# One split instruction a weight slab on ScalarE and one on VectorE, in place of two halves on each

## The chip, the cores and the metric

The kernel runs on one core of a Trainium2 chip. The metric is the device time of one launch in microseconds (us). Three launches of the kernel before were timed, and one execution was profiled.

## The reference

Two blocks of a network over 256 tokens with 1024 features each, in float32. What matters here is that nearly everything is a product of activations with a weight matrix that is used once, from an "even" mixer (attention and gated linear attention), a feed-forward unit (width 2816), an S5 mixer, eight experts of width 2816 (two for each token), and then the second block with another feed-forward unit, an SSD mixer, neighbourhood attention and per-layer embeddings:

```python
def adaln(c, w, b):
    m = jax.nn.silu(c.astype(jnp.float32)) @ w + b
    shift, scale, gate = jnp.split(m, 3, axis=-1)
    return shift[:, None, :], scale[:, None, :], gate[:, None, :]
...
def swiglu(h, w_gate, w_up, w_down):
    return (jax.nn.silu(h @ w_gate) * (h @ w_up)) @ w_down

def moe_swiglu(h, w_router, w_gate, w_up, w_down):
    logits = (h @ w_router).astype(jnp.float32)
    top_val, top_idx = lax.top_k(logits, TOP_K)
    weights = jax.nn.softmax(top_val, axis=-1)
    gates = jnp.sum(jax.nn.one_hot(top_idx, N_EXPERTS, dtype=jnp.float32) * weights[..., None], axis=-2)
    out = jnp.zeros_like(h)
    for e in range(N_EXPERTS):
        out = out + gates[..., e:e + 1] * swiglu(h, w_gate[e], w_up[e], w_down[e])
    return out
```

The products have to be as exact as float32 products.

## The kernel before

Activations lie with features on the 128 partitions and 256 tokens along the free axis. TensorE (PE) multiplies in the float32r type, so a float32 operand is cut into two parts, hi and lo (12 bits each, by the class's docstring), and each product is three matmuls (`mm3`: w hi by act hi, w hi by act lo, w lo by act hi).

The weights come through the class `Stream` as about 525 slabs of 128 x 2048 float32 (1 MB each), in the order of their use. A slab goes through three steps:

- `_load`: the SyncE queue (SP) issues a DMA into a raw buffer `wraw` (3 of them; during the experts 2 more, `wraw2`). A buffer is free for the next load when the split of the slab in it has read it for the last time.
- `_prep`: ScalarE (ACT) writes hi with an `activation` Copy, which rounds into the float32r tile `whi` (line 211), and VectorE (DVE) writes lo = raw - hi into `wlo` (line 212). Both are done in two halves of 1024 columns. There are 3 pairs of whi and wlo.
- the products (lines 269 and 271), in `proj`, `proj_tok`, `ffn`, `Down` and `moe_block`. Nearly all read a slab k by k, so that the first products need the first half of a slab alone.

The same engines do the rest of the work. In a feed-forward unit, each of 11 segments takes three slabs (gate g, up u and down d), and ACT and DVE make `gu` and its split `mh`, `ml` between the products. In the experts, each of 8 times 11 = 88 segments takes three slabs too. For segment s, PE makes the gate and up products, ACT the Silu `mt` (line 1655), DVE its product with up (line 1656), PE transposes it into `ms`, ACT and DVE split that into `mmh` and `mml` (lines 283 and 284), and PE makes the down products of the segment before. POOL has work in the mixers and at the ends of units.

The kernel is written in a framework that orders the instructions of each engine when the program is built: a planner with a clock of its own gives each engine's next place to the instruction of the highest priority among those that are ready by that clock. Priority is program order, moved by `high_priority(offset=...)`; `SPLIT_ORDER` moves the splits of some units by a few places. On the chip each engine then runs its list in that fixed order and waits, at each instruction, for what it depends on. An edit in `_prep` so changes what the planner sees for every slab. A name of a tile in the rows is that of the code; `hgx` is the activations that an expert works on.

Of the kernel before, what the change touches and what calls it, by code (L numbers as in the profile page):

```python
# [28 lines left out]
# How much earlier (or later) than in program order the parts of a weight slab are made, by the unit that takes it.  # L29
SPLIT_ORDER = {"s": -30, "f1_0": -100, "e": -200, "f2_0": 50}  # L30

# Vectors over features, one column of 128 partitions for each 128 features: name, input, columns.
# [10 lines left out]
def lay_out(inp):  # L43
    """The inputs as the kernel reads them: features on partitions, weights in the pieces that are loaded."""
    inp = {k: np.asarray(v) for k, v in inp.items()}

    def part(w, k=None):
        """[k * 128, n] -> [128, k, n]"""
        return w.reshape(-1, 128, w.shape[-1]).transpose(1, 0, 2)

    def cut(w, ranges):
        """columns of a matrix, 256 to a piece: [piece, 128, k, 256]"""
        return np.stack([part(np.concatenate([w[:, a:b] for a, b in r], 1)) for r in ranges])
# [4 lines left out]
    def tok(w, c0):  # L58
        """512 columns, in two pieces of 512 rows: [piece, 128, 4, 512]"""
        return np.stack([part(w[s * 512:(s + 1) * 512, c0:c0 + 512]) for s in range(2)])  # L60

    f = np.float32
# [26 lines left out]
    # columns on partitions: [piece, 128, 2, rows]  # L89
# [19 lines left out]
    # rpb[h, row distance, column distance] for each query column (twice, for two rows) and key column  # L109
# [7 lines left out]
def rows(w, k0, k1):  # L117
    """Rows of a matrix on partitions: [128, k1 - k0, columns]."""
    return w[k0 * 128:k1 * 128, :].rearrange("(k p) c -> p k c", p=128)
# [7 lines left out]
class Stream:  # L127
    """Weights in the order of their use. Loads run NR slabs ahead of the split into two
    float32r parts (exact: 12 + 12 bits), and the split runs NH slabs ahead of the products."""
# [19 lines left out]
    def grow(self, pool, n, until, limit=None):  # L149
        """n more loads at a time, into another pool, for what comes before slab (or key) `until`"""  # L150
        self.pool2, self.more, self.turn = pool, n, self.turn % self.NR
        self.until = until if isinstance(until, int) else self.key.get(until, len(self.plan))
        self.advance(limit)

    def once(self, pool, *names):
        """room for one more load each"""
# [37 lines left out]
    def _prep(self, i):  # L194
# [10 lines left out]
        m = n // 2  # L205
        k0 = self.plan[i][0]
        k0 = k0[0][0] if isinstance(k0[0], tuple) else k0[0]
        for c in range(0, n, m):
            cs = slice(c, c + m)
            with self.K.tc.high_priority(offset=SPLIT_ORDER[k0]) if k0 in SPLIT_ORDER else nullcontext():  # L210
                nc.scalar.activation(hi[:, cs], t[:, cs], AF.Copy)  # L211
                nc.vector.tensor_sub(lo[:, cs], t[:, cs], f32(hi[:, cs]))  # L212
# [34 lines left out]
class Kernel:  # L247
# [12 lines left out]
    # ------------------------------------------------------------ small helpers  # L260
# [3 lines left out]
    def first(self):  # L264
        """what comes within goes before other work that is ready at the same time"""
        return self.tc.high_priority(offset=200)
# [4 lines left out]
    def mm3(self, out, w, act, start, stop):  # L271
        """out += w.T @ act for float32 operands given as (high, low) float32r parts."""
# [4 lines left out]
    def tr(self, out, in_, o=0):  # L277
        """transpose of in_, whose first partition is o"""
# [10 lines left out]
    # ------------------------------------------------------------ constants  # L289
# [23 lines left out]
    # ------------------------------------------------------------ modulation  # L313
    def silu_row(self):
        """silu(c) as a row, on every partition"""
# [5 lines left out]
    def silu_c(self, pool):  # L321
        """silu(c) on partitions, each on its own with 31 columns of zeros, and room for partial sums"""
# [7 lines left out]
    def mod_plan(self, name, norm, part, pe):  # L330
        """shift | scale | gate of one sublayer: the matrix times silu(c), on PE with its rows on partitions (partial
        sums are then added over partitions on PE as well), or on DVE with its columns on partitions. part: which third."""
# [43 lines left out]
    def mod_flush(self, keep, norm=None):  # L376
        """what the last slabs of modulation matrices have left to do, but for the last few (and for what does not
        belong to that norm's first two thirds)"""
# [3 lines left out]
    def mod_next(self, n=None):  # L382
        """the next loads of modulation matrices go into the stream here"""
# [4 lines left out]
    # ------------------------------------------------------------ norms over features  # L388
# [5 lines left out]
    def norm_begin(self, pool=None):  # L394
        """pool: where a folded norm's h goes"""
# [4 lines left out]
    def sums(self, tag="ss"):  # L400
        """sums of squares of feature tiles: a tile, and those of the last pair, which are not added to it"""
        return [self.act.tile([128, T], F32, name=tag, tag=tag, bufs=1)]

    def sq_add(self, p, src, ss, gain=None, last=3):
        """adds the squares of two feature tiles (times a gain)"""
# [15 lines left out]
    def norm_part(self, p, g):  # L421
        """x[2p], x[2p+1] are final: their squares, and x * g in two parts"""
# [10 lines left out]
    def rstd_from(self, v, r):  # L433
        """r = 1 / sqrt(v), with one Newton step"""
# [14 lines left out]
    def col_sums(self, out, ss):  # L449
        """per token, tokens on partitions"""  # L450
# [5 lines left out]
    def rstd_cols(self, ss, n, b):  # L456
        """1 / rms of each token, tokens on partitions: [128, 2]"""
# [8 lines left out]
    def to_rows(self, r, b):  # L466
        """[128, 2] over tokens -> the same row of 256 tokens on every partition, in PSUM"""
# [18 lines left out]
    def mod_norm(self, norm, row=None, pre=None):  # L486
        """h = x * rstd * (gain * (1 + scale)) + shift, in two parts; squares were added up before. pre: products
        x * gain * (1 + scale) that were taken before"""
# [27 lines left out]
    # ------------------------------------------------------------ products  # L516
    def proj(self, keys, evac, k_outer=False, K=KD, act=None):
        """Columns of h @ w on partitions; evac(tile, out) per 128 columns, two tiles to a bank."""
# [26 lines left out]
    def proj_tok(self, keys, evac, act=None, per=4, mid=None):  # L545
        """h @ w with tokens on partitions, 512 columns: keys are slabs of `per` row tiles each; mid is called after the first."""
# [21 lines left out]
    class Down:  # L568
        """out.T over 8 feature tiles, accumulated over row tiles of w that come in pairs"""
# [22 lines left out]
    # ------------------------------------------------------------ residuals  # L592
# [13 lines left out]
    # ------------------------------------------------------------ feed forward  # L606
    def ffn_plan(self, key, gate, up, down, between=0, mid=None):
        """between: how many loads of modulation matrices go with each segment; mid: plans other work in the midst"""
# [14 lines left out]
    def ffn(self, key, tail, fold, end=None, mid=None):  # L623
        """fold: h is x * gain and 1/rms (from end) goes onto the products; else h is normalised"""
# [59 lines left out]
    # ------------------------------------------------------------ first block, layer 0: FoX + GLA  # L684
# [21 lines left out]
    def even_consts(self, pool, tmp):  # L706
        """Loads and masks of the mixer that wait for nothing"""
# [6 lines left out]
        # which head a row of the small product stands for  # L714
# [12 lines left out]
        # causal mask, to be added: 0 where s <= t, else very low  # L727
# [4 lines left out]
        # 1 where the running sum goes on, 0 where a chunk of 64 begins  # L732
# [4 lines left out]
        # level masks [s, t]: t in the second half of a block of 2m, s in the first half of the same one  # L737
# [8 lines left out]
        for i, sh in enumerate((6, 5, 4, 3, 2, 1, 0)):  # L746
            # t >> sh == (s >> sh) + 1 and (s >> sh) even  <=>  (t >> sh) ^ (s >> sh) == 1 and t > s
# [9 lines left out]
    def log_sigmoid(self, out, x, t, scale):  # L757
        """out = scale * log_sigmoid(x); t: a spare tile"""
# [7 lines left out]
    def even_mixer(self, pool, tail):  # L766
        nc, tc, E = self.nc, self.tc, self.E
        # the gates' small products first: their chain is the longest
# [26 lines left out]
        # log decays of GLA, summed within chunks of 64  # L795
# [11 lines left out]
        # FoX forget gates, summed over time  # L807
# [5 lines left out]
        # FoX queries and keys  # L813
# [10 lines left out]
        # GLA: decays between halves of blocks of 128, 64, ..., 2 steps, each from a point between the two,  # L824
        # so that no exponent is above 0
# [5 lines left out]
        def decay(m):  # L831
            """exp(-|b - b at the last step of the first half|)"""
# [42 lines left out]
        def lv_chunk():  # L875
            # over chunk boundaries: from the start of a later chunk, to the end of an earlier one
# [11 lines left out]
            # chunks 0, 1 -> 2, 3: also over the whole of chunk 1, of chunk 2  # L888
# [22 lines left out]
        # ---- FoX  # L911
# [3 lines left out]
        def fox_scores(hd):  # L915
# [12 lines left out]
            # minus the masked logits, and minus their maximum  # L928
# [56 lines left out]
        # ---- GLA out, normalised over its 128 features; the products of FoX's half with w_o come between  # L985
# [33 lines left out]
    # ------------------------------------------------------------ first block, layer 1: S5  # L1019
# [12 lines left out]
    def poly_exp(self, pool, x, out, m1=None):  # L1032
        """out = exp(x), m1 = exp(x) - 1, to float32's accuracy, for [128, 32] tiles"""
# [24 lines left out]
    def poly_trig(self, pool, th, sn, vs):  # L1058
        """sn = sin(th), vs = 1 - cos(th), for [128, 32] tiles"""
# [22 lines left out]
        for _ in range(2):  # L1082
            # sin 2y = 2 sin y (1 - v), 1 - cos 2y = 2 sin(y)^2
# [5 lines left out]
    def s5_tables(self, pool, rot, tmp):  # L1089
        """What depends on the parameters alone. State (g % 2, p) on partitions, pair g // 2 on columns."""  # L1090
# [15 lines left out]
        # a - 1 = (mag - 1) - mag (1 - cos)  # L1106
# [17 lines left out]
        # decay and turn of two steps  # L1124
# [16 lines left out]
        def cmul(pr_, pi_, xr, xi, cr, ci, neg=False):  # L1141
            """(pr, pi) = (xr, xi) * (cr, ci), the second over columns; neg: of conjugates"""
# [9 lines left out]
        # input weights f * b, and times a: [state, feature tile, re or im, pair, (a b, b), k]  # L1152
# [6 lines left out]
        # output weights re, -im, and those times a  # L1159
# [1349 lines left out]
```

## Time and profile before

| | |
|---|---|
| three launches | 2844.84, 2849.65 and 2849.4 us; median 2849.4 us |
| the profiled execution | span 2843.7 us; no device time of its own is listed, so what lies around its span is bounded by the launches: 1.1 to 6.0 us |
| PE, DVE, ACT, POOL busy | 2671.7, 2181.9, 1579.6 and 560.9 us |
| weight splits | 1046 instructions on ACT (1044.7 us) and 1046 on DVE (1282.3 us) |
| DMA | 623 MB, a mean of 219 GB/s |

Engines work side by side, so busy times don't add up to the span. A matmul's record and the next one's overlap, so PE's time is read from starts, not from durations. An engine that is idle costs nothing unless the work that ends last waits for it.

### The profile page before, as it was taken

What the parts mean: (1) busy time and instruction counts of PE and PEld (TensorE: products, weight loads), DVE (VectorE), ACT (ScalarE), POOL (GpSimd) and SP (SyncE); (2) the same over time, 40 slices, a digit from 0 to 9 for tenths busy, and PEclk for the clock granted to TensorE, in tenths of its full rate; (3) what the DMA queues carried; (4) which work ended last, traced back from release to release, by engine and by line L of the source; (5) the groups of instructions that cost most, each with busy time, mean ns of one, the idle gap of its engine ahead of it and who ended that gap; (6) DMA issues with size and microseconds to landing.
All of it is one profiled execution on the core that took longest, in us unless ns stands there. A gap on an engine that the chain in (4) does not pass through costs nothing. (4 is left out here: it accounts for less than half of the span.)

```text
span 2843.7 us, 50584 instructions
## 1 busy us (share of the span) xinstructions
PE 2671.7 (94%) x20739; PEld 2496.3 (88%) x20739; DVE 2181.9 (77%) x3100; ACT 1579.6 (56%) x2222; POOL 560.9 (20%) x490
## 2 busy tenths in 40 slices
PE   8999978989999999999998998887899999999999
PEld 6789967789999999998778997887899999978999
DVE  6989986879998998888775568999665665665656
ACT  5344336557777777777663445666444444465444
POOL 2413982310000000000000005766100010240000
PEclk9999988989999999999999999998999999999999
DMA  7476863348999999989763544444345545552553
GB/s 272 165 269 250 285 213 124 123 178 298 342 343 343 334 344 363 330 326 357 246 213 131 183 166 150 149 148 149 134 178 192 180 163 183 188 194 77 185 183 119
DMA packets 109210, 623.17 MB, mean 219 GB/s; under 512 B 10048, under 2 KB 10064, under 8 KB 56352
## 3 DMA queue, kind: packets, MB, share of 16 engines
q1 hardware_dynamic: 107664, 612.05, 60.2%
q0 software_dynamic: 1296, 7.68, 0.7%
q8 instruction: 169, 2.77, 0.4%
q14 instruction: 81, 0.66, 0.1%
HBM read 616.49 MB, written 3.21 MB: 218 GB/s over the span
## 5 line engine op out<-in xcount | busy, mean ns | idle before, releaser
L212 DVE TENSOR_TENSOR wlo<-wraw,whi 128x1024 fp32r<-128x1024 f32 (+1 forms) x1046 | 1282.3, 1263 | 252.5 <-ACT whi L211 249.9
L211 ACT ACTIVATE whi<-wraw 128x1024 fp32r<-128x1024 f32 (+1 forms) x1046 | 1044.7, 1048 | 695.7 <-issue 381.4
L269 PE MATMUL pj<-hh,whi 128*128 128x256 f32 (+1 forms) x2672 | 768.8, 288 | 55.4 <-DVE czb L1924 34.9
L269 PE MATMUL pj<-hh,wlo 128*128 128x256 f32 (+1 forms) x2672 | 766.4, 287 | 2.8 <-DVE wlo L212 2.8
L269 PE MATMUL pj<-hl,whi 128*128 128x256 f32 (+1 forms) x2672 | 767.7, 287 | 1.2 <-DVE hl L287 1.2
L269 PEld LDWEIGHTS pj<-hh,whi 128*128 128x128 f32 (+1 forms) x2672 | 517.3, 194 | 60.4 <-issue 28.7
L269 PEld LDWEIGHTS pj<-hh,wlo 128*128 128x128 f32 (+1 forms) x2672 | 515.5, 193 | 5.3 <-DVE wlo L212 4.3
L269 PEld LDWEIGHTS pj<-hl,whi 128*128 128x128 f32 (+1 forms) x2672 | 515.1, 193 | 2.8 <-DVE hl L287 2.2
L269 PE MATMUL pj<-whi,hg 128*128 128x256 f32 x2112 | 389.9, 281 | 0.0
L269 PEld LDWEIGHTS pj<-whi,hg 128*128 128x128 f32 x2112 | 328.0, 188 | 11.2 <-issue 8.7
L269 PE MATMUL pj<-wlo,hg 128*128 128x256 f32 x1056 | 295.9, 280 | 0.0
L269 PE MATMUL acc<-mh,whi 128*128 128x256 f32 x880 | 245.4, 279 | 13.7 <-ACT whi L211 13.7
L269 PE MATMUL acc<-mh,wlo 128*128 128x256 f32 x880 | 245.8, 279 | 5.1 <-DVE wlo L212 5.1
L269 PE MATMUL acc<-ml,whi 128*128 128x256 f32 x880 | 245.3, 279 | 0.4 <-DVE ml L284 0.4
L269 PEld LDWEIGHTS pj<-wlo,hg 128*128 128x128 f32 x1056 | 198.6, 188 | 3.5 <-issue 2.1
L269 PEld LDWEIGHTS acc<-mh,whi 128*128 128x128 f32 x880 | 167.0, 190 | 13.9 <-ACT whi L211 13.9
L416 POOL TENSOR_TENSOR ss<-sq 128x256 f32<-128x256 f32 x11 | 11.9, 1082 | 845.0 <-ACT sq L409 607.8
L440 POOL TENSOR_TENSOR rc<-var,mhalf 128x2 f32<-128x2 f32 x2 | 1.4, 704 | 894.1 <-DVE var L1796 892.8
L269 PEld LDWEIGHTS acc<-mh,wlo 128*128 128x128 f32 x880 | 166.7, 189 | 6.2 <-DVE wlo L212 6.2
L269 PEld LDWEIGHTS acc<-ml,whi 128*128 128x128 f32 x880 | 166.8, 190 | 0.6 <-DVE ml L284 0.6
L269 PE MATMUL acc<-wlo,mmh 128*128 128x512 f32 x352 | 139.7, 397 | 0.0
L269 PE MATMUL acc<-whi,mml 128*128 128x512 f32 x352 | 138.7, 398 | 0.7 <-DVE mml L284 0.7
(721 smaller groups left out, 4424.9 us busy)
## 6 DMA issues: line engine op xcount, KB each, us to landing
wraw<-in_o_exp_down_dram SPq DMA_DIRECT2D x88, 1024.0 KB, 5.3
wraw<-in_ffn_w_gu_dram SPq DMA_DIRECT2D x88, 1024.0 KB, 4.9
wraw<-in_o_exp_gate_dram SPq DMA_DIRECT2D x87, 1024.0 KB, 5.4
wraw<-in_o_exp_up_dram SPq DMA_DIRECT2D x87, 1024.0 KB, 5.4
wraw<-in_ffn_w_down_dram SPq DMA_DIRECT2D x44, 1024.0 KB, 5.0
wraw<-in_ssd_cols_dram SPq DMA_DIRECT2D x32, 1024.0 KB, 4.9
wraw<-in_e_mod_ffn_w_t_dram SPq DMA_DIRECT2D x12, 1024.0 KB, 4.9
wraw<-in_o_mod_mix_w_t_dram SPq DMA_DIRECT2D x12, 1024.0 KB, 5.0
```

The costliest lines, as they stand in the source:

```text
L211: nc.scalar.activation(hi[:, cs], t[:, cs], AF.Copy)
L212: nc.vector.tensor_sub(lo[:, cs], t[:, cs], f32(hi[:, cs]))
L269: self.nc.tensor.matmul(out, lhsT, rhs, start=start, stop=stop, skip_group_check=True)
L416: nc.gpsimd.tensor_add(ss[0], sq[:, 0, :], sq[:, 1, :])
L440: nc.gpsimd.tensor_tensor(r, v, self.mhalf.to_broadcast([128, n]), op=OP.pow)
```

## The change

`_prep` issues one activation over all columns of a slab and one subtraction over all columns, in place of two each. Both stand in one `high_priority` block as before. The number of buffers, their sizes, the loads and the products are the same. A product of the first half of a slab now depends on an instruction that writes the whole slab. The rest of the diff takes out comments and docstrings.

```diff
         hi = self.pool.tile([128, self.size], FR, name="whi", bufs=self.NH)
         lo = self.pool.tile([128, self.size], FR, name="wlo", bufs=self.NH)
-        m = n // 2
         k0 = self.plan[i][0]
         k0 = k0[0][0] if isinstance(k0[0], tuple) else k0[0]
-        for c in range(0, n, m):
-            cs = slice(c, c + m)
-            with self.K.tc.high_priority(offset=SPLIT_ORDER[k0]) if k0 in SPLIT_ORDER else nullcontext():
-                nc.scalar.activation(hi[:, cs], t[:, cs], AF.Copy)
-                nc.vector.tensor_sub(lo[:, cs], t[:, cs], f32(hi[:, cs]))
+        with self.K.tc.high_priority(offset=SPLIT_ORDER[k0]) if k0 in SPLIT_ORDER else nullcontext():
+            nc.scalar.activation(hi[:, :n], t[:, :n], AF.Copy)
+            nc.vector.tensor_sub(lo[:, :n], t[:, :n], f32(hi[:, :n]))
         self.split[i] = (hi, lo)
```

## Rows read from the trace of the kernel before

**Rows 1.** The page, busy time of each engine (share of the span, instructions).

```profile
PE 2671.7 (94%) x20739; PEld 2496.3 (88%) x20739; DVE 2181.9 (77%) x3100; ACT 1579.6 (56%) x2222; POOL 560.9 (20%) x490
```

**Rows 2.** Windows: stretch, PE, PEld, DVE, ACT, POOL busy, granted clock, DMA share, GB/s.

```profile
213.00:430.00 217.00, 195.02 (x1577) 192.46 (x1575) 198.75 (x285) 80.01 (x95) 159.36 (x114) 0.96 0.70 247
...
655.00:1425.00 770.00, 768.58 (x5626) 699.78 (x5624) 679.96 (x788) 561.84 (x721) 0.00 (x0) 1.00 0.91 332
...
1706.00:1991.00 285.00, 233.48 (x1851) 223.47 (x1849) 265.53 (x312) 176.83 (x212) 192.97 (x163) 0.91 0.42 148
```

**Rows 3.** PE's waits, whole span: us in total, times, longest.

```profile
PE pj L269 <- DVE czb L1924: 45.2, 7, 10.3
PE acc L269 <- ACT whi L211: 13.7, 1, 13.7
...
PE acc L269 <- DVE wlo L212: 5.1, 5, 1.9
...
PE pj L269 <- DVE wlo L212: 2.8, 6, 0.7
```

**Rows 4.** Groups by form, whole span: count | busy, mean ns | idle before.

```profile
L211 ACT ACTIVATE whi<-wraw 128x1024 fp32r<-128x1024 f32 x1042 | 1043.1, 1051 | 692.5 <-issue 378.2 <-PE pj L269 167.6 <-PE acc L269 65.4
...
L283 ACT ACTIVATE mh<-gu 128x512 fp32r<-128x512 f32 x55 | 34.0, 618 | 17.3 <-DVE gu L642 17.3
...
L212 DVE TENSOR_TENSOR wlo<-wraw,whi 128x256 fp32r<-128x256 f32 x2 | 0.8, 418 | 0.0
```

**Rows 5.** Groups by form, the experts (655 to 1425 us).

```profile
L212 DVE TENSOR_TENSOR wlo<-wraw,whi 128x1024 fp32r<-128x1024 f32 x485 | 570.0, 1220 | 65.9 <-ACT whi L211 64.0
```

**Rows 6.** Timeline, experts, late order: start us, us, engine, line [idle before].

```profile
885.92 0.39 ACT L1655 ACTIVATE mt<-pj 128x256 f32<-128x256 f32 x1 [2.51 <-PE pj L269]
...
903.43 0.39 ACT L1655 ACTIVATE mt<-pj 128x256 f32<-128x256 f32 x1 [2.27 <-PE pj L269]
...
903.72 2.00 ACT L211 ACTIVATE whi<-wraw 128x1024 fp32r<-128x1024 f32 x2
...
904.80 2.36 DVE L212 TENSOR_TENSOR wlo<-wraw,whi 128x1024 fp32r<-128x1024 f32 x2 [0.53 <-ACT whi L211]
...
906.37 0.28 PE L269 MATMUL pj<-wlo,hgx 128*128 128x256 f32 x1
...
1334.24 0.38 ACT L1655 ACTIVATE mt<-pj 128x256 f32<-128x256 f32 x1 [2.13 <-PE pj L269]
```

**Rows 7.** Windows of the wlo instructions alone: stretch, DVE busy (count), clock, DMA.

```profile
284.00:430.00 146.00, 67.35 (x44) 0.94 0.70 246
...
1706.00:1991.00 285.00, 93.91 (x62) 0.91 0.42 148
```

**Rows 8.** Timeline of a feed-forward unit of the second block.

```profile
2158.38 2.35 DVE L212 TENSOR_TENSOR wlo<-wraw,whi 128x1024 fp32r<-128x1024 f32 x2
...
2167.99 0.28 PE L269 MATMUL pj<-hh,whi 128*128 128x256 f32 x1
```

**Rows 9.** Timeline, experts, early order (a split of g ahead of mt).

```profile
865.04 2.01 ACT L211 ACTIVATE whi<-wraw 128x1024 fp32r<-128x1024 f32 x2 [0.71 <-PE pj L269]
...
871.11 0.28 PE L269 MATMUL pj<-wlo,hgx 128*128 128x256 f32 x1
```

**Rows 10.** The page, DMA issues: count, KB each, median us to landing.

```profile
wraw<-in_o_exp_down_dram SPq DMA_DIRECT2D x88, 1024.0 KB, 5.3
```

**Rows 11.** Timeline of PE at the first slabs.

```profile
41.86 0.58 PE L269 MATMUL pj<-hh,wlo 128*128 128x256 f32 x1 [0.49 <-DVE wlo L212]
```

**Rows 12.** Timeline of DVE in the SSD mixer.

```profile
1971.11 4.30 DVE L212 TENSOR_TENSOR wlo<-wraw,whi 128x1024 fp32r<-128x1024 f32 x2
```

**Rows 13.** Timeline of ACT at the end of the first feed-forward unit.

```profile
413.87 0.22 ACT L328 ACTIVATE silz<-vecs 128x8 f32<-128x8 f32 x1 [19.94 <-POOL silz L327]
413.98 3.88 ACT L211 ACTIVATE whi<-wraw 128x1024 fp32r<-128x1024 f32 x4
```

## The prediction

> **What bounds the kernel now.** I read the busy times first, then windows by stage, PE's waits, the groups of the two split lines, and timelines where a slab is used soon after it is split. PE is busy 94% of the span and DVE 77% [rows 1]. The share hides three kinds of stage. In the experts PE is busy 768.58 of 770 us, and DVE has 90 us to spare; in the first feed-forward unit and in the SSD mixer DVE is busy 92% and 93% and PE waits [rows 2]. What the change touches, PE's wait for a split, is small today: 13.7 us once for whi, and 5.1 and 2.8 us in eleven waits for wlo; the largest wait, 45.2 us, is for another result of DVE [rows 3]. So little can be won at PE by faster splits, and much can be lost if they come later.
>
> **What one slab costs.** ACT's half is 1051 ns; from 512 to 1024 columns the two copies differ by 433 ns, so a whole slab is 1.051 + 2 x 0.433 = 1.92 us [rows 4]. DVE's half is 1220 ns where nothing disturbs it, 128x256 takes 418 [rows 4, 5], so 1.044 ns a column, and the whole is 1.220 + 1.069 = 2.29 us. Two halves that follow each other take 2.00 us on ACT and 2.36 on DVE [rows 6], since the second starts before the first's record ends. The change so saves 0.08 us of ACT and 0.07 us of DVE a slab: over some 523 slabs 42 and 37 us of busy time, of which only what lies on the path counts.
>
> [...]
>
> **What is later.** In the late order of the experts, the split of g starts on ACT at 903.72, DVE's first half at 904.80 (ACT's 1.05 and 0.03 of hand-over), and is done 1.23 us on, 2.31 after ACT began; the second half 3.44 after [rows 6]. Merged, hi is ready after 1.92 and lo after 1.92 + 0.03 + 2.29 = 4.24. The first lo product so can start 1.93 us later than now, the last 0.80 later, and the raw buffer comes free 0.80 later.
>
> **Where DVE is full.** 44 halves fall into the first feed-forward unit and 62 into SSD [rows 7]: 53 slabs x 0.07 = 3.7 us saved, if DVE is the path there throughout; bounds 0 and 3.7. I take 3.7.
>
> **Feed-forward units.** The halves end at 2160.73 and PE begins on that slab at 2167.99 [rows 8]. 0.80 later changes nothing; 6.5 us are left. Cost 0. Without that cover each of the 33 slabs of a unit would cost up to 1.93.
>
> **The experts, early order.** The split of g starts at 865.04, ahead of mt, and PE wants lo at 871.11 [rows 9]: done at 865.04 + 4.24 = 869.28, 1.8 us are left. Cost 0. The buffers: two segments take 17.51 us, from the mt at 885.92 to that at 903.43 [rows 6], so one takes 8.76 for its three slabs, and five buffers make a round of 14.6 us; landing takes 5.3 [rows 10] and a split 4.24, so 0.80 later is covered by the 5 that remain.
>
> **The experts, late order.** From 885.92 to 1334.24, 50 of the 88 segments run mt first (behind 2.27 us of idle time, for PE's last up product) and the split of g behind it [rows 6]. The first lo half is done at 906.03 and PE uses it at 906.37: 0.34 us of cover. In the same order the merged lo is done at 903.72 + 4.24 = 907.96, and PE, which runs in its fixed order, stands for 1.59 us, in every segment, because mt waits for PE and the split for mt. That would be 50 x 1.59 = 80 us. But the order is not fixed across the edit. ACT sits idle for 2.27 us just ahead of mt while the raw slab is a buffer's round old; I infer that the planner put mt first because by its clock the slab and mt came up close to each other. With the merged split, products end later on that clock by the 1.93 us by which lo comes later, mt becomes ready later with them, and the load does not. So I expect the split of g ahead of mt, as in the early order, and take 0; the bounds are 0 and 80.
>
> **The other waits for lo.** Eleven waits at most 1.93 longer: bounds 0 and 21.2. The one at 41.86, at the start, where little else is under way, I take whole, 1.9 [rows 11]. The other ten I put in the stretches where DVE is full, and there lo's time is set by DVE's sum of work, not by the latency of one slab; DVE's idle share of 8% [rows 2] of 10 x 1.93 is 1.5. In SSD the halves follow each other with no idle time ahead of them (1971.11, 4.30 us for both [rows 12]), which speaks for the low end.
>
> **Larger pieces on DVE.** Other work that comes up during a slab now finds 2.29 us ahead of it, in place of 1.22: 1.1 more at most. The seven waits for czb [rows 3] bound it at 7.7, below 0. Halves mostly follow each other already, so I take 2.
>
> **ACT's one long wait.** The activation of silz waits 19.94 us for POOL, and four halves stand behind it; they start at 413.98, and PE waits 13.7 us for them [rows 3, 13]. Where it stands is the planner's choice again. Between -13.7 (a split goes ahead of it) and +6.2 (one more slab behind it without cover: 1.92 on ACT and the 4.30 that two halves take on DVE beside POOL's work [rows 12]) I take 0.
>
> **The sum.** -3.7 + 0 + 0 + 1.9 + 1.5 + 2 + 0 = +1.7 on the profiled span of 2843.7: 2845.4. The median of the launches lies 5.7 above that span, so the time is **2851 us**. Its own range is 2841 (all costs at nothing, -3.7, and 4.6 for the spread of the three launches) to 2870 (half of the bound of waits and all of the pieces).
>
> **Rivals.**
>
> *The late order stays.* Then 50 segments lose 1.59 us: 2851 + 80 = 2931; if half of them keep it, 2891. For it: the rows show that order with 0.34 us of cover. Against it: what I said on the planner, and that 38 segments already run otherwise. It decides from the point where, in a segment like that at 903.72, ACT begins the split of g later than 906.37 - 4.24 = 902.13. [...] Chance 0.25.
>
> *A gain.* The splits behind silz go ahead of it and the 13.7 us vanish: 2851 - 13.7 = 2837. For it: ACT is idle 19.94 us there, and every ready slab could be split in that time. Against it: nothing in the edit moves the POOL memset, and the planner, which put the splits behind, evidently saw no such wait. Chance 0.15, together with other gains from a new order.
>
> *Nothing can be seen.* It is contained in the forecast: if all terms are 0, 2849.
>
> **Chances and range.** The forecast 0.60, the late order 0.25, the gain 0.15. A measurement of this kernel can tell about 0.2% (5.7 us) from no change, so "the same" is 2843.7 to 2855.1. Of the forecast I put 0.05 below, 0.31 within and 0.24 above (the waits near their bound); of the gain 0.11 below and 0.04 within; all of the late order above. Faster 0.16, the same 0.35, slower 0.49. The range for 8 in 10 reaches from 2836 (the gain) to 2940 (the late order in most segments).
>
> **What would show it.** ACT and DVE busy fall by some 42 and 37 us, with 523 instructions fewer on each; groups of 128x2048 at 1.92 and 2.29 us. In the experts PE stays near 769 of 770 us, and ACT's timeline has the split of g ahead of mt in all segments. Wrong in the first place would be a large wait of PE for wlo (line 209 or so) in the experts, a stage of 800 us or more there, or mt followed at once by the split of g. Wrong in the small terms: PE's waits for wlo outside the experts grow by much more than 3.4 us, or the 13.7 us for whi are gone or larger.

## The result, and the profile after

The changed kernel takes 2886.4 us (median of four launches, 2883.1 to 2889.3), the kernel before, beside it, 2849.5: a ratio of 1.0126, 95% interval 1.0108 to 1.0145, so 37 us slower. The profiled span grew by 41.2 us, from 2843.7 to 2884.9; the execution that was profiled before is one of its shorter ones, so the stages below add up to some 4 us more than the medians differ by. Of all launches in this document one, at 2975 us with a granted clock of 0.83 in place of 0.96 to 0.97, is left out of its kernel's median and ratio.

The first part of the page after shows what the change does by itself; it answers to [rows 1].

```profile
PE 2701.5 (94%) x20739; PEld 2511.4 (87%) x20739; DVE 2118.9 (73%) x2575; ACT 1538.8 (53%) x1697; POOL 572.2 (20%) x490
```

The splits got cheaper, as forecast: ACT is busy 40.8 us less (42 forecast) and DVE 63.0 less (37 forecast), with some 525 instructions fewer on each. None of it arrived at the end. The groups by form in the experts give the price of a whole slab, 1915 and 2290 ns, against 1.92 and 2.29 us forecast from [rows 4, 5]:

```profile
L209 DVE TENSOR_TENSOR wlo<-wraw,whi 128x2048 fp32r<-128x2048 f32 x223 | 508.6, 2290 | 81.8 <-ACT whi L208 81.3
L208 ACT ACTIVATE whi<-wraw 128x2048 fp32r<-128x2048 f32 x223 | 426.9, 1915 | 64.1 <-PE pj L266 51.6 <-PE acc L266 11.0
```

PE's waits over the whole span, to be held against [rows 3]:

```profile
PE pj L266 <- DVE czb L1921: 31.2, 7, 6.6
PE pj L266 <- DVE wlo L209: 17.6, 16, 2.2
...
PE acc L266 <- ACT mh L280: 12.4, 1, 12.4
...
PE acc L266 <- DVE wlo L209: 6.7, 6, 2.1
```

The waits for wlo went from 7.9 us in eleven to 24.3 in 22. That is 16.4 of 41.2 us, less than half. To see where the rest is, I cut the span at three events that every kernel has: the first Silu of the experts (mt), the first extra product of the experts' last turn (mhx), and the first Silu of the second block's feed-forward units (gu, line 637 or 634). The view is that of one tile: count, shortest, median and longest ns, and the first and last start in us. Before:

```profile
L1655 ACT ACTIVATE mt<-pj x88: 359/385/388, 648.1 to 1479.4; 128x256 f32<-128x256 f32 x88
```

```profile
L269 PE MATMUL acc<-wraw,mhx x352: 379/379/403, 1338.1 to 1467.3; 128*32 128x256 f32 x176
```

```profile
L637 ACT ACTIVATE gu<-gu x44: 614/617/634, 1524.9 to 2798.5; 128x512 f32<-128x512 f32 x44
```

And after:

```profile
L1652 ACT ACTIVATE mt<-pj x88: 360/385/388, 658.1 to 1509.0; 128x256 f32<-128x256 f32 x88
```

```profile
L266 PE MATMUL acc<-wraw,mhx x352: 379/379/403, 1357.0 to 1497.0; 128*32 128x256 f32 x176
```

```profile
L634 ACT ACTIVATE gu<-gu x44: 612/615/634, 1561.3 to 2837.1; 128x512 f32<-128x512 f32 x44
```

Differences of these starts give four stages. Ahead of the experts 658.1 against 648.1 us (+10.0), the experts up to the last turn 698.9 against 690.0 (+8.9), the last turn and what follows it up to the second block's Silu 204.3 against 186.8 (+17.5), and the rest 1323.6 against 1318.8 (+4.8). The biggest piece is in a stage in which PE waits for no split.

What happened to the orders is seen in ACT's timeline. This is a segment of the experts after (mmh is the high part of ms, the transposed product of the segment):

```profile
913.58 3.91 ACT L208 ACTIVATE whi<-wraw 128x2048 fp32r<-128x2048 f32 x2
918.46 0.39 ACT L1652 ACTIVATE mt<-pj 128x256 f32<-128x256 f32 x1 [0.96 <-PE pj L266]
918.74 1.91 ACT L208 ACTIVATE whi<-wraw 128x2048 fp32r<-128x2048 f32 x1
922.07 0.38 ACT L280 ACTIVATE mmh<-ms 128x256 fp32r<-128x256 f32 x1 [1.42 <-PE ms L277]
```

The two splits ahead of mt are those of d and g; the one behind it is that of u. By the trace 41 of the 88 segments had mt, g, mmh, u, d on ACT before; after, none has, and 46 have mt, u, mmh, d, g (an expectation below counts 40 of these). The late order of [rows 6] is gone, as forecast.

And this is PE in a segment of the last turn, after. Here places 128 to 159 of the turn are multiplied by the raw slab in full float32, in products that use 32 of the array's 128 columns (mhx with the gate and up weights, mmx with the down weights):

```profile
1440.62 0.44 PE L277 MATMUL ms<-ident,mt 128*128 128x128 f32 x2
1440.99 1.04 PE L266 MATMUL pj<-wraw,mmx 128*32 128x512 f32 x2
1441.96 0.50 PE L266 MATMUL acc<-whi,mmh 128*128 128x512 f32 x1
1442.30 0.40 PE L266 MATMUL acc<-wlo,mmh 128*128 128x512 f32 x1
1442.54 0.39 PE L266 MATMUL acc<-whi,mmh 128*128 128x512 f32 x1
1442.77 0.40 PE L266 MATMUL acc<-wlo,mmh 128*128 128x512 f32 x1
1443.10 1.06 PE L266 MATMUL pj<-wraw,mmx 128*32 128x512 f32 x6
```

Before, the same products stood together:

```profile
1431.57 1.06 PE L269 MATMUL pj<-wraw,mmx 128*32 128x512 f32 x8
1432.57 0.39 PE L269 MATMUL pj<-whi,hg 128*128 128x256 f32 x1
```

A float32 matmul leaves two records here (352 for the code's 176 mhx products), so eight records are a group of four. From the first start to the start of what follows, four on different columns take 1.0 us together. Torn into one and three, they take 0.97 and 0.99. Nine of the eleven groups are torn after, none before. A segment of the last turn is longer by 1.5 us; before:

```profile
1443.39 0.38 ACT L1655 ACTIVATE mt<-pj 128x256 f32<-128x256 f32 x1
...
1456.40 0.38 ACT L1655 ACTIVATE mt<-pj 128x256 f32<-128x256 f32 x1
```

and after:

```profile
1455.53 0.38 ACT L1652 ACTIVATE mt<-pj 128x256 f32<-128x256 f32 x1
...
1470.03 0.38 ACT L1652 ACTIVATE mt<-pj 128x256 f32<-128x256 f32 x1
```

The question for the experiments was therefore: how much is the later readiness of whole slabs, and how much is the new order that the planner wrote, above all PE's.

### The profile page after: what moved, and what is told of

The parts are those of the page before. It is cut to its first block, busy times and chain, and to the rows that moved or that the text cites. A ratio compares the mean times of both kernels' runs of the same rounds, so it can differ in the third digit from the quotient of the medians.

```text
span 2884.9 us, 49549 instructions
## 1 busy us (share of the span) xinstructions
PE 2701.5 (94%) x20739; PEld 2511.4 (87%) x20739; DVE 2118.9 (73%) x2575; ACT 1538.8 (53%) x1697; POOL 572.2 (20%) x490
## 5 line engine op out<-in xcount | busy, mean ns | idle before, releaser
L209 DVE TENSOR_TENSOR wlo<-wraw,whi 128x2048 fp32r<-128x2048 f32 (+1 forms) x523 | 1206.0, 2311 | 359.7 <-ACT whi L208 358.7
L208 ACT ACTIVATE whi<-wraw 128x2048 fp32r<-128x2048 f32 (+1 forms) x523 | 997.7, 1909 | 775.2 <-PE pj L266 314.9
L266 PE MATMUL acc<-mh,whi 128*128 128x256 f32 x880 | 245.4, 279 | 12.4 <-ACT mh L280 12.4
L266 PE MATMUL acc<-whi,mmh 128*128 128x512 f32 x352 | 138.8, 404 | 2.0 <-ACT mmh L280 2.0
```

The lines of the kernel that those rows point to most:

```text
L208: nc.scalar.activation(hi[:, :n], t[:, :n], AF.Copy)
L209: nc.vector.tensor_sub(lo[:, :n], t[:, :n], f32(hi[:, :n]))
L266: self.nc.tensor.matmul(out, lhsT, rhs, start=start, stop=stop, skip_group_check=True)
```

## The experiments

**The order and the split apart.** The planner orders anew at every edit, so an edit alone can't tell its own cost from that of the order. These kernels write the order out: each engine's instructions, numbered as the program issues them, are chained in a stored order by dependencies that ask for no semaphore.

```diff
             Kernel(tc, aps, ctx).build(out, Kernel.UNITS)
+            pin(tc, nc, ORDER)      # for each engine: its instructions in a stored order
...
+        for a, b in zip(order, order[1:]):
+            tc.add_manual_dep(b, a.name, mybir.DependencyInfo(mybir.DependencyClass.NoSync, mybir.DependencyReason.DATA), reason="pin")
```

First, merged splits in the order of the kernel before:

> Merged splits, but every engine's instructions pinned to the order of the kernel before (each merged split at the place of its first half); nothing is left out. If the new order alone makes the time (theory 1: the planner's order), this runs like the kernel before: 2845 to 2855 us. If the later readiness of a whole slab is what costs (theory 2: latency at a fixed order), the 50 segments of the experts in the late order lose 1.59 us each, and the time is 2849 + 80 = about 2930 us, 2915 to 2950, with a stage of the experts some 80 us longer and PE waiting for wlo in it.

Second, halves in the order of the changed kernel:

> Splits in halves, every engine's instructions pinned to the order of the changed kernel (the two halves of a slab one behind the other at the place of its merged split); nothing is left out. Theory 1 (order): it keeps the loss, 2874 to 2888 us; what it is below 2886 is what whole slabs cost at that order, at most the some 20 us that PE there waits for wlo. Theory 2 (latency): halves bring it back to 2845 to 2857 us.

Measured: 3001.0 us for the first (ratio 1.0524, 1.0509 to 1.054) and 2872.8 for the second (1.0079, 1.0064 to 1.0093). With before and after this makes a square:

| us | halves | merged | merged less halves |
|---|---|---|---|
| order of before | 2850.5 | 3001.0 | +150 |
| order of after | 2872.8 | 2886.4 | +14 |
| new order less old | +22 | -115 | |

Both theories hold a part. At the old order whole slabs cost 150 us, and in the late segments the loss is the one that could be worked out from [rows 6]. From the timeline of the first of these kernels, ACT:

```profile
1163.24 0.38 ACT L1652 ACTIVATE mt<-pj 128x256 f32<-128x256 f32 x1 [3.82 <-PE pj L266]
...
1173.60 0.39 ACT L1652 ACTIVATE mt<-pj 128x256 f32<-128x256 f32 x1 [4.06 <-PE pj L266]
```

and PE:

```profile
1167.81 0.39 PE L266 MATMUL pj<-wlo,hg 128*128 128x256 f32 x1 [1.49 <-DVE wlo L209]
```

A segment takes 10.36 us; 8.76 + 1.59 = 10.35 were forecast. In total the experts up to the last turn grew by 106.5 us, more than the 80 of the 50 late segments, and the part ahead of the experts by 30.9, so the price of this rival was set too low. On the mean of the 41 segments in that order the loss is 1.76 us each. Segments that the prediction had at no cost lose as well: twelve of the early ones take 0.73 us more each (mt at 693.5, 703.0 and 712.5 us, before at 661.5, 670.2 and 678.8). The planner's new order takes nearly all of it back. With halves it costs 22 us by itself: the same instructions, in another order.

**Which stage owes what to which.** Where the last turn alone is left in halves, and where it alone is merged:

```diff
-        m = n // 2
+        m = n // 2 if self.plan[i][0][:2] == ("m", 7) else n      # the second kernel: n and n // 2 exchanged
```

> Merged splits everywhere but for the slabs of the experts' last turn, which are split in halves; ordered anew by the planner; nothing is left out. Its written order is that of the changed kernel up to that turn, and none of the fours is torn. Theory (the last turn's order makes some 17 of the 37 us): 2886 - 17 = 2869 us, with segments of that turn of 13.0 us as before. Rival (that turn is long for what came ahead of it): 2880 to 2890 us.

> The reverse: merged splits in the experts' last turn alone, halves elsewhere; ordered anew by the planner; nothing is left out. Its written order is that of the kernel before up to that turn, with nine fours torn in it. Theory (the last turn's order makes some 17 us wherever it is entered from): 2850 + 17 = 2867 us, segments of 14.5 us there. Rival: 2848 to 2855 us.

Measured: 2868.3 us (1.0074, 1.0056 to 1.0092) and 2871.4 us (1.0073, 1.0053 to 1.0092), both within 5 us of what the theory gave. By the same three events, the growth of each stage over the kernel before:

| us over before | ahead of the experts | experts to last turn | last turn to second block | rest |
|---|---|---|---|---|
| changed kernel | +10.0 | +8.9 | +17.5 | +4.8 |
| halves, order of after | +3.3 | +4.5 | +15.8 | +4.4 |
| merged but for the last turn | +8.3 | +9.0 | +2.7 | +2.5 |
| merged in the last turn alone | +0.1 | +0.1 | +18.9 | +8.6 |
| merged, order of before | +30.9 | +106.5 | +12.7 | +9.1 |

What is merged in one stage leaves the time of the others nearly as it was, by the two kernels in the middle. In the order of after, the last turn's 16 to 19 us are there with halves (+15.8) as with whole slabs (+17.5, +18.9). But the order is not all of it. At the order of before, where no group of mmx is torn, whole slabs make the same turn 12.7 us longer. There PE waits for mtx, a short DVE instruction for the extra places; on DVE its input msx now stands behind a whole subtraction. First merged splits in the order of before, then the kernel before:

```profile
PE ms L277 <- DVE mtx L1606: 9.9, 11, 1.3
```

```profile
PE ms L280 <- DVE mtx L1609: 0.6, 1, 0.6
```

So for merged splits the new order costs 4.8 us here over the old one, and wins 118 ahead of this turn. The last column also moves by 3 to 8 us in kernels that have the very order and splits of before there (below), so I read nothing from it.

**Why that turn is longer.** First the torn groups, in the changed kernel's own order: the torn one is moved back to its three.

> The changed kernel with its own order, but for nine matmuls of PE in the experts' last turn: the products of the extra places with the down weights come in fours, nine of the eleven fours are torn into one and three with other matmuls between them, and here the one is moved next to its three; nothing is left out. Theory 1a (a torn four takes PE twice, about 0.53 us more in each of its two passes): 9 x 1.06 = 9.5 us less, 2877 us. Rival (PE time in that turn is the same however the matmuls are ordered, and the turn is longer for another reason): 2886 us.

Measured: 2881.5 us (1.0108, 1.0093 to 1.0122), between the two. The stage says more than the time: 204.4 us, where the changed kernel has 204.3, so the 5 us lie elsewhere in the span. Within the stage, the turn itself (from the first mhx product to the last mmx product) takes 153.3 us in place of 155.8, and what follows it 51.1 in place of 48.5; that last part also differs by 4 us among kernels that share the order of before there (47.9 to 51.9). So 2.5 us were won in the turn, of 9.5 expected. PE's timeline shows what came in place of the pass that was saved:

```profile
1436.44 0.44 PE L277 MATMUL ms<-ident,mt 128*128 128x128 f32 x2
...
1437.55 0.50 PE L266 MATMUL acc<-whi,mmh 128*128 128x512 f32 x1 [0.68 <-ACT mmh L280]
```

In this order the down products follow the transposes whose result they need, and the torn one had stood in the gap while ACT made mmh. In this stage PE waits ten times for mmh, 6.3 us, in the changed kernel twice, 0.7. So theory 1a fell as it was put. It could still be right that a torn group costs a pass, with a wait hiding that here. That was tried from both sides. In the kernel before, in its own order, a group is torn as in the changed one, or groups of eight mhx products, which already stand torn in two in nine segments (in five of them into five and three), are put together:

> The kernel before with its own order, but for PE in the experts' last turn: in nine segments the first of the four extra products with the down weights is moved ahead of four other matmuls, so that the four is torn into one and three as in the changed kernel; nothing is left out. Theory 1a: segments of 13.0 us become 14.0 (0.52 for each of its two passes), and the time 2850 + 9 x 1.0 = 2859 us. Rival: segments stay at 13.0 and the time at 2850.

> The kernel before with its own order, but for PE in the experts' last turn: in nine segments two transposes stand within an eight of the extra products with the gate or up weights (five, two transposes, three), and here they stand behind it; nothing is left out. Theory 1a (products on a quarter of the array's columns run four at a time, and a torn group costs PE another pass of about 0.5 us): segments of 13.0 us become 12.5, and the time 2850 - 9 x 0.5 = 2845 us. Rival (what PE gives up is waited for elsewhere in the segment): segments stay at 13.0 and the time at 2850.

Measured: 2862.2 us torn (1.0039, 1.0026 to 1.0053) and 2843.9 us put together (0.9971, 0.9959 to 0.9984). Segments, torn:

```profile
1449.98 0.39 ACT L1655 ACTIVATE mt<-pj 128x256 f32<-128x256 f32 x1
...
1464.17 0.39 ACT L1655 ACTIVATE mt<-pj 128x256 f32<-128x256 f32 x1
```

and put together:

```profile
1414.72 0.39 ACT L1655 ACTIVATE mt<-pj 128x256 f32<-128x256 f32 x1
...
1427.19 0.39 ACT L1655 ACTIVATE mt<-pj 128x256 f32<-128x256 f32 x1
```

14.19 and 12.47 us, where the kernel before takes 13.01: +1.18 for a torn four and -0.54 for a mended eight. Back in the changed kernel, the three are now moved to the one, into the gap:

> The changed kernel with its own order, but for PE in the experts' last turn: where a four was torn into one and three, the three are moved ahead, next to the one, which stands between the transposes into ms and the down products that wait for ScalarE's mmh; nothing is left out. In the earlier run, with the one moved back to its three, PE waited 0.68 us for mmh in each segment, at the place the one had left. If the torn one had only filled that wait, a whole four at that place fills it and pays no pass twice: segments of 14.5 us become 13.4 (0.5 for each of two passes), and the time 2886 - 9 x 1.06 = 2877 us. Rival (the gain of 4.9 us of the earlier run is all that this order gives): 2881 us, segments of 14.2.

Measured: 2876.7 us (1.0087, 1.0072 to 1.0103), as the theory had it; the stage is 195.1 us, 9.2 less than the changed kernel's, and a segment 13.32:

```profile
1448.15 0.38 ACT L1652 ACTIVATE mt<-pj 128x256 f32<-128x256 f32 x1
...
1461.47 0.39 ACT L1652 ACTIVATE mt<-pj 128x256 f32<-128x256 f32 x1
```

So a little more than half of the stage's 17.5 us is the torn groups. In the turn itself (first mhx to last mmx product) they are more: 138.8 us before, 155.8 after, 144.8 here, so 11.0 of 17.0. The kernel before with torn groups agrees, 149.2 us, 10.4 more than without. Of the 6.0 us that remain in the turn, 2.0 are one wait of PE for mmx at its end, which the kernel before has not; for the rest I have no run that takes it apart. Behind the turn 2.3 us remain, within what that part differs by among kernels of one order.

**Which of the two engines.** One part of the change alone, each ordered anew. The first kernel's edit against before is shown; the second has the activation in the loop, and one subtraction behind it:

```diff
-        for c in range(0, n, m):
-            cs = slice(c, c + m)
-            with self.K.tc.high_priority(offset=SPLIT_ORDER[k0]) if k0 in SPLIT_ORDER else nullcontext():
-                nc.scalar.activation(hi[:, cs], t[:, cs], AF.Copy)
+        with self.K.tc.high_priority(offset=SPLIT_ORDER[k0]) if k0 in SPLIT_ORDER else nullcontext():
+            nc.scalar.activation(hi[:, :n], t[:, :n], AF.Copy)
+            for c in range(0, n, m):
+                cs = slice(c, c + m)
                 nc.vector.tensor_sub(lo[:, cs], t[:, cs], f32(hi[:, cs]))
```

> One activation over the whole slab, but two subtractions, ordered anew by the planner; nothing is left out. In its written order 27 segments of the experts still run mt first and the split of g behind it, 20 the other way, and no four of the extra products is torn. The first lo half is ready 1.92 + 0.03 + 1.23 = 3.18 us after ACT's start, 0.87 later than in halves. Theory (where the late order stays, cover of 0.34 us decides): 27 x 0.53 = 14 us in the experts and none in the last turn: 2864 us, 2857 to 2872. Rival (any new order costs some 20 us, as the changed kernel's does): the last turn is some 15 us longer too, 2870 to 2885.

> Two activations, but one subtraction over the whole slab, ordered anew by the planner; nothing is left out. lo is ready 2.00 + 0.03 + 2.29 = 4.32 us after ACT's start, as late as in the changed kernel. Its written order has the split of g ahead of mt in 40 segments (as in the changed kernel), and four of the eleven fours of the last turn torn. Theory (lo's readiness and the order it makes are the whole of the change, and ACT's part adds nothing): most of the changed kernel's loss, 2870 to 2888 us. Rival (the later hi is what costs): 2848 to 2858 us.

Measured: 2863.1 us (1.0055, 1.0038 to 1.0072) and 2880.9 us (1.0105, 1.0082 to 1.0129), both as the theory had it. In the first, late segments have at their shortest the length that their cover gives, 8.76 + 0.53 = 9.29 (the median of the 27 is 9.42):

```profile
1099.06 0.39 ACT L1655 ACTIVATE mt<-pj 128x256 f32<-128x256 f32 x1 [2.98 <-PE pj L269]
...
1108.35 0.39 ACT L1655 ACTIVATE mt<-pj 128x256 f32<-128x256 f32 x1 [2.98 <-PE pj L269]
```

Its experts up to the last turn are 22.0 us longer, not 14. PE waits there for 11.6 us, 8.6 of them for wlo in 23 waits; where the other 10 us come from is not shown. DVE's whole subtraction by itself, with the order that it brings, makes most of the loss (32.5 us of 37).

**A version that beats both.** The profile showed two small things in the kernel before: the wait behind silz, and the torn eights. The first alone, then both:

> The kernel before with its own order, but ScalarE's activation of silz is moved behind eighteen later instructions, so that the splits behind it no longer wait for POOL; nothing is left out. If the 13.7 us that PE waits there for whi are on the path: 2836 to 2841 us. Rival (DVE, or the end of the feed-forward unit, is the path there, and the wait is only moved): 2845 to 2850 us.

> The kernel before with its own order and both small moves: the transposes behind the eights, and the activation of silz behind eighteen later instructions; nothing is left out. If the two add up: 3.9 us less by the second, as measured, and 4.5 by the first: 2842 us, below both kernels. Rival (the first move brings nothing): 2847 us.

Measured: 2846.6 us for the first (0.9981, 0.997 to 0.9992), and 2840.5 for both (0.9969, 0.9956 to 0.9982): with halves, and 9.6 us under the kernel before. The first alone won 3.9 us, so its rival held: most of the 13.7 us of PE's wait were not on the path. Without it PE waits there for what DVE and ACT make:

```profile
PE acc L269 <- DVE ml L284: 3.3, 2, 2.1
PE ms L269 <- ACT sq L409: 3.0, 1, 3.0
PE acc L269 <- DVE wlo L212: 1.7, 1, 1.7
```

These two kernels and the one with the eights put together share the order of before from the second block on, and by the same events their rest is 8.4, 5.5 and 3.1 us longer than in the profile before. That is the scatter of that column. (The first one's profiled execution, 2853.2 us, was the slowest of its twelve.)

## Why the prediction was right or wrong

The time lies in the range, 2836 to 2940, but outside the range of the likeliest case, 2841 to 2870, and 35 us above the forecast. "Slower" had 0.49 of the chance. That the range holds it is luck: it reaches so high for the rival of the late order, which did not come, and the loss that came is another one.

- **The experts, late order.** Right in mechanism, and in size for the segment shown. The split of g went ahead of mt, and at the old order that segment costs 1.60 us more (1.59 forecast), the mean of the 41 1.76; the 50 of the prediction are those of the stretch, and by the trace 45 of them had g behind mt. That the planner moved g for the reason given is not shown. The step "I take 0" was off by 8.9 us; with halves in the same order 4.5 of these remain, so about half of it is the order and half the later slabs. Most of the order's half goes with PE's granted clock, which in this order stands at 0.50 for 6.8 us while PE is busy: by an estimate 3.4 us (last section).
- **The step that failed.** The sum has a term for ACT's order and none for PE's. The prediction said that the order is not fixed across the edit, and then asked only where that would hurt or help the split. The last turn is 15.8 to 18.9 us longer in the three kernels with the new order there, and 9 to 11 of these are torn groups. The rows that were read could not price it, but a stage with a second kind of product, of which four take 1.0 us together, could have been looked for. Nor does the sum price a later split in that turn: its late segments end at 1334.24, and at the old order whole slabs cost 12.7 us behind that.
- **The other waits for lo.** Mis-sized: 3.4 us were taken of a bound of 21.2, and PE's waits for wlo grew by 16.4. Ahead of the experts whole slabs cost 10.0 - 3.3 = 6.7 us at one order (4.3 and 5.1 by the two kernels that share the changed one's order and splits there).
- **Larger pieces on DVE.** 2 us were taken, within a bound from the waits for czb alone. These fell, by 14.0 us, and at the old order it is another small instruction, mtx, that PE waits 9.9 us for.
- **Where DVE is full.** The saving was mis-sized as well, the other way. Two windows of the wlo instructions alone, which answer to [rows 7]:

```profile
291.00:438.00 147.00, 53.60 (x22) 0.93 0.70 247
...
1743.00:2028.00 285.00, 78.50 (x31) 0.91 0.41 144
```

  DVE won 13.8 and 15.4 us there, 0.6 and 0.5 us a slab in place of 0.07. Elsewhere the trace agrees with a small saving: two whole slabs that follow each other take 4.49 us in the experts, two pairs of halves 4.62, 0.06 us a slab. It bought little: PE's wait for czb, in the second stretch, fell by 14.0 us, and the stage ahead of the experts, which holds the first, grew.
- **Feed-forward units of the second block.** Right. The four units and what lies between them, from the first gu to the last, take 1275.8 us, before 1273.6.
- **silz.** Right: it stayed where it was, and PE waits 12.4 us (for mh, which stands behind it on ACT) in place of 13.7.
- **Waits for wlo in the experts.** In the kernel pinned to the order of before whole pieces make PE wait 73.4 us for wlo in 66 waits from 920 to 1480 us (1.49 in the segment shown). With the planner free that is mostly ordered away (2.3 us in three waits from 655 to 1470 us), and the loss has another form.

That the new order, and in it the torn groups, makes most of what was missed is shown by runs that add up. Not settled are some 4 of the 17.0 us of the last turn, the part of whole slabs ahead of the experts, and what brings the clock down in the experts.

## What to carry to other kernels

When a planner writes the order, an edit of one instruction is an edit of all engines' lists. Compare the written orders first, and pin one to price the edit and the order apart: here +150 and -115 hid behind +37. A cover read from one segment (what is ready when, what needs it when) was good to 0.01 us for a segment like it and to 0.2 us on the mean, as long as the order held. And look for products that take hardly longer together than alone (here four in 1.0 us, one in 0.97): other matmuls between them made a segment 1.18 us longer.

## What was unexpected of the hardware

Four float32 products on a quarter of the array's columns each take about 1.0 us together, and one alone takes as long as three (0.97 and 0.99 us).

The gain of a merged subtraction goes with what POOL does: 0.06 us a slab where POOL is idle, 0.6 in a stretch in which POOL is busy 90% of the time and 0.5 in one in which it is busy 65 to 68%. No run changes POOL's work alone, so the cause is not shown.

In the changed kernel PE's granted clock fell at a change of experts, while PE had been busy without a break; columns are PE, PEld, DVE, ACT, POOL busy, granted clock, DMA share, GB/s:

```profile
1250.00:1254.00 4.00, 4.00 (x26) 3.42 (x24) 3.58 (x3) 2.57 (x3) 0.00 (x0) 1.00 0.86 318
1254.00:1258.00 4.00, 4.00 (x25) 3.90 (x26) 1.00 (x3) 2.56 (x4) 0.00 (x0) 0.70 1.01 388
1258.00:1262.00 4.00, 4.00 (x15) 3.52 (x15) 2.29 (x1) 0.80 (x2) 0.00 (x0) 0.50 0.36 107
1262.00:1266.00 4.00, 4.00 (x28) 3.68 (x28) 1.15 (x2) 3.04 (x3) 0.00 (x0) 0.95 0.60 240
```

At 0.50 PE began 15 matmuls in 4 us, and 28 in the next 4. The kernel before shows 1.00 at its change there. It goes with the order: with halves in the order of after the granted clock is 0.78 from 1240 to 1250 us and 0.70 in the next 4, which is 6.8 us at 0.50 if the rest is at 1.00, as long as the changed kernel has 0.50 (1255.6 to 1262.4 us). With PE busy throughout, 3.4 us are lost by that (an estimate: half of 6.8). What differs ahead of it are the products that gather the extra places, 32 of them, with outputs of 32 columns each. After, they stand in runs of 17, 11 and 4:

```profile
1253.07 2.05 PE L266 MATMUL acc<-mPx,htok 128*128 128x32 f32 x17
...
1255.16 2.11 PE L266 MATMUL acc<-mPx,htok 128*128 128x32 f32 x11
```

and the clock falls at 1255.6. Before, they are spread over 22 us, in runs of at most ten:

```profile
1238.96 1.18 PE L269 MATMUL acc<-mPx,htok 128*128 128x32 f32 x10
```

That they bring the clock down is not shown: no run moves them alone.
